# Gated delta rule over two blocks of 128 tokens instead of four chunks of 64, in a streamed-weight decoder layer

## The chip, the cores and the metric

The kernel is one launch on one NeuronCore of a Trainium2 chip. Its engines are TensorE (PE), VectorE (DVE), ScalarE (ACT), GpSimd (POOL) and SyncE (SP), which issues every DMA here. The metric is the device time of that launch in microseconds (us).

## The reference

One decoder layer with batch 1, 256 tokens, width 2048: three residual branches, each fed by a norm that a conditioning vector `c` scales and shifts, and a last norm.

```python
x = x + 0.5 * gt1 * swiglu(ada_in(x, norm_g[0], sh1, sc1), wg[0], wu[0], wd[0])
x = x + gt2 * hybrid_mixer(ada_in(x, norm_g[1], sh2, sc2), w_in, w_out, ...)
x = x + 0.5 * gt3 * swiglu(ada_in(x, norm_g[2], sh3, sc3), wg[1], wu[1], wd[1])
return rmsnorm(x, final_norm)
```

The mixer has 8 heads of softmax attention with a forget gate (FoX) and 8 heads of the gated delta rule, all 128 wide. The delta rule, in chunks of `c` tokens (64 in the reference; the size of the chunk does not change what is computed):

```python
lower = where(strict, (kb @ k.T) * decay, 0)          # per chunk, c x c
t_inv = inverse(eye + lower)
u, w = t_inv @ vb, t_inv @ (kb * exp(g))
a = where(incl, (q @ k.T) * decay, 0)
# over the chunks, in order
v_new = u - w @ state
o = (q * exp(g)) @ state + a @ v_new
state = state * exp(g_last) + (k * exp(g_last - g)).T @ v_new
```

## The kernel before

**The weight stream.** All weights are read once, as 674 blocks of eight 128x128 tiles. For a block, SP issues a DMA of 512 KB (`wraw`), ACT casts it to `whi` (L129), DVE makes the rest `wlo = wraw - whi` (L141), and PE multiplies each tile with the activations in three products, high by high, high by low and low by high (L815 to L817 in the mixer's projections, `pp`; L828 to L830 for those with tokens in the rows, `pv`; L500 to L511 and L591 to L593 in the two feed-forward parts). These products fill PE from end to end. Between weights DVE also computes the conditioning vector's product with its own matrix (`adat`, L267, 142 pieces).

**The mixer's small work.** What the heads need beside the projections is written as Python generators: `gates`, `decays`, `keys`, `solve`, `gdn` (one head of the delta rule), `fox` (one head of attention), `to_out`. `yield 1.4` asks that 1.4 us of stream pass before the generator goes on; each tile of the stream calls `tick(TILE_US)` with 0.35. So between two tiles PE gets a few small fp32 products, called a visit here, with results in one of three PSUM banks (`pss`) and the next visit far enough behind for DVE or ACT to have answered. The Tile framework's scheduler then orders each engine's instructions; `tc.issue_after` pins one behind another.

**One delta head before** (`gdn`, L1047). `solve` inverts the 16x16 diagonal blocks of four heads at once on DVE (L1023, L1024), writes the result to DRAM and reads it back turned (`lt`, L1029; `x<-lt`, L1033, into a part of `x[:, 7]`), and spreads it over masked 64-wide tiles `U0` (L1037). Then `gdn` doubles the inverse twice, 16 to 32 to 64: `pu` (or `put`) holds `U` transposed and `L @ U`; ACT and DVE copy the one half each into `Tm` (L1072, L1073), DVE masks the other into `Z` (L1078), and `pn = Tm.T @ Z` (L1101, L1121) is added to `U`. With the 64-blocks known, `puw` (L1129, L1130) gives `u` and `w`, and a chain goes over four chunks: `po<-st,wq` (L1149), `vz` on DVE (L1150), `po<-vz,At` (L1152), `pst` (L1155), the new state `st` on DVE (L1160). `orw` (L1164, L1165) collects the output.

**Rows of decays.** `fetch_rows` (L941, `x<-rowd`) spreads four heads' rows of cumulated decay over all partitions, into `x[:, 0:4]` or `x[:, 4:8]`, which are free inside the mixer; `decays` makes the masked `Ln` of them (L950, L953). In attention `plog` (L1203) holds logits, DVE takes their maximum `fmx` (L1208, L1210), ACT the exponents (L1212), PE turns the result (`ppt`, L1217) and multiplies it with `v` (`pfo`, L1223 to L1225); its output goes out through `pft` (L1239).

**Norms and end.** `norm_sums` sums squares over partitions on PE (`nsum`, L337) and makes the reciprocal root (L343 to L348); `rb`/`nrow` (L356, L357) spread it, `ht` (L384) and `hs` (L395) give the modulated activations, column by column through `h_upto`. `W.held` is a list of instructions behind which the coming `wlo` are pinned, one each. At the end `final` transposes x back (`pout`, L1350), scales it with the last norm (L1355, L1356) and stores it in four DMAs (L1357).

Of the kernel before, what the change touches and what calls it, by code (L numbers as in the profile page):

```python
# [8 lines left out]
F32 = mybir.dt.float32  # L9
# [20 lines left out]
EPS = 1e-6  # L30
WB = 8
# [125 lines left out]
def layer_kernel(ctx: ExitStack, tc: tile.TileContext, xrow, c, adaw, cols, cst, w, out, order, dbg=None):  # L157
# [77 lines left out]
    ident = L("ident")  # L235

# [92 lines left out]
    def norm_sums(between=lambda _: None, end=lambda _: None):  # L329
# [14 lines left out]
        V.tensor_scalar(hv, ps[:, 0:4:2], -0.5 / D, -0.5 * EPS, ALU.mult, ALU.add)  # L344
# [182 lines left out]
    def residual(ps, j, m_gt, half, one=False):  # L527
# [6 lines left out]
        i = V.scalar_tensor_tensor(x[:, j], ps[:, :T], g, x[:, j], ALU.mult, ALU.add)  # L534
# [112 lines left out]
    def ffn(which, m_gt, early=None):  # L647
        fs = list(range(NF))
        with tc.tile_pool(name=f"hid{which}", bufs=PARTS[which][1] + HIDX) as hp, \
                tc.tile_pool(name=f"more{which}", bufs=1) as more:  # L650
            W.more = more if MORE else None
            for half in range(2):
# [7 lines left out]
                def after(j):  # L660
                    residual(pds.pop(j), j, m_gt, True, half == 1 and j == KD - 1)
# [46 lines left out]
    def features(i):  # L708
# [4 lines left out]
        def moved():  # L713
            return A.copy(x[:, 2 * i : 2 * i + 2], px.rearrange("p (a t) -> p a t", a=2)).ins
# [24 lines left out]
    with tc.issue_after(hold):  # L739
        hold = A.activation(fy, fv, AF.Sqrt, bias=L("eps"), scale=1.0 / D).ins  # L740
    V.tensor_scalar(fh, fv, -0.5 / D, -0.5 * EPS, ALU.mult, ALU.add)
# [33 lines left out]
    def mixer():  # L775
# [67 lines left out]
        U0 = gp.tile([P, NH, 2, 64], F32, name="U0")  # L843

        def gates(ps):
# [42 lines left out]
            for t in range(2):  # L888
                sl = slice(t * P, (t + 1) * P)
                PE.matmul(pr[:NH, T + t * P : T + (t + 1) * P], y[:, t, gdn_], C("tri64"), start=True, stop=True)  # L890
# [3 lines left out]
            for t in range(2):  # L894
                PE.matmul(pcs[:, t, 1], C("tri64"), y[:, t, gdn_], start=True, stop=True)
                PE.matmul(pcs[:, t, 2], C("tru64"), y[:, t, gdn_], start=True, stop=True)
# [8 lines left out]
            V.tensor_tensor(nbeg, colS[:, :, 4], colS[:, :, 2], ALU.mult)  # L905
            V.tensor_scalar(nbt, colS[:, :, 4], -1.0, None, ALU.mult)
            V.tensor_scalar(ng, colS[:, :, 1], -1.0, None, ALU.mult)
# [12 lines left out]
        bh = lambda c_, n: c_.unsqueeze(1).to_broadcast([n, 2, 64])  # L920

        def decay(h):
# [8 lines left out]
            A.activation(gb, gb, AF.Exp)  # L931
            return dd, gb
# [41 lines left out]
        def keys(h):  # L974
# [14 lines left out]
            A.copy(kT[:, 1], pk[:, :T])  # L989
# [7 lines left out]
        def solve(half):  # L997
# [33 lines left out]
            U = x[:, 7, :P].rearrange("p (n i) -> p n i", n=n)  # L1031
            with tc.issue_after(W.last):
                nc.sync.dma_start(U, lt[ht].rearrange("n b (q i) -> (b q) n i", q=16))  # L1033
            yield 5.0
            for q in range(2):
                with tc.issue_after(W.split):
                    V.tensor_tensor(  # L1037
                        U0[:, hs4].rearrange("p h t (b i) -> p (h t) b i", b=4)[:, 4 * q : 4 * q + 4],
                        U[:, 4 * q : 4 * q + 4].unsqueeze(2).to_broadcast([P, 4, 4, 16]),
                        C("blk").unsqueeze(1).unsqueeze(3).to_broadcast([P, 4, 4, 16]), ALU.mult)  # L1040
# [6 lines left out]
        def gdn(h):  # L1047

            kT, q_ = kk.pop(h).bitcast(F32), qv.pop(h).bitcast(F32)
            dec, egb = ups.pop(h)  # L1050
            L_, U = Ln[:, h], U0[:, h]
            yield 5.0 if h < NH - 2 else 3.0

            pv = pss("pvq")
            pg = pss("pkq")
            pu = pss("pu0")
            for t in range(2):
                sl = slice(t * P, (t + 1) * P)
                PE.transpose(pu[:64, sl], U[:, t], ident)
            for t in range(2):  # L1060
                PE.matmul(pu[:, T + t * 64 : T + (t + 1) * 64], L_[:, t], U[:, t], start=True, stop=True)
            for t in range(2):
                sl = slice(t * P, (t + 1) * P)
                PE.transpose(pv[:, sl], q_[:, 1, sl], ident)
                PE.transpose(pv[:, T + t * P : T + (t + 1) * P], q_[:, 0, sl], ident)
            for t in range(2):
                sl = slice(t * P, (t + 1) * P)
                PE.matmul(pg[:, sl], kT[:, 0, sl], q_[:, 0, sl], start=True, stop=True)

            def factor(i, p_):  # L1070
                v_ = p_[:64, :T].rearrange("p (t i) -> p t i", t=2)
                A.copy(Tms[i][:64, :, :64], v_[:, :, :64])  # L1072
                V.tensor_copy(Tms[i][64:, :, 64:], v_[:, :, 64:])  # L1073
                return Tms[i]

            def masked(l, p_):
                Z = m1p.tile([P, 2, 64], F32, name="Z")
                V.tensor_tensor(Z, p_[:, T : T + P].rearrange("p (t i) -> p t i", t=2), bh(C("zm", 64 * l, 64), P), ALU.mult)  # L1078
                return Z

            Tm = factor(0, pu)
            Z = masked(0, pu)

            ssq = tiny.tile([P, 2], F32, name="ssq")
            kbd = m1p.tile([P, 2, 2, P], F32, name="kbd")
            kb, kd = kbd[:, 0], kbd[:, 1]
            vb = m1p.tile([P, 2, P], F32, name="vb")
            At = m1p.tile([P, 2, P], F32, name="At")
            V.tensor_tensor(At, pg[:, :T].rearrange("p (t i) -> p t i", t=2), dec, ALU.mult)
            for t in range(2):  # L1090
                sl = slice(t * P, (t + 1) * P)
# [3 lines left out]
                A.activation(kb[:, t], kT[:, 1, sl], AF.Copy, scale=rb2[:, t, h : h + 1])  # L1095
                A.activation(kd[:, t], kT[:, 1, sl], AF.Copy, scale=colS[:, t, 3, h : h + 1])
            V.tensor_scalar(ssq, ssq, EPS, EPS * HD, ALU.add, ALU.mult)
            yield 1.6
            pn = pss("pn")
            for t in range(2):  # L1100
                PE.matmul(pn[:, t * 64 : (t + 1) * 64], Tm[:, t], Z[:, t], start=True, stop=True)  # L1101
            U2 = m2p.tile([P, 2, 64], F32, name="U")
            V.tensor_tensor(U2, pn[:, :P].rearrange("p (t i) -> p t i", t=2), U, ALU.add)
            U = U2

            wq = m1p.tile([P, 2, 4, 64], F32, name="wq")
            V.tensor_tensor(wq[:, :, 0:4:3, :], q_[:, 0].rearrange("p (t c i) -> p t c i", t=2, c=2),
                            egb.rearrange("p (t c i) -> p t c i", t=2, c=2), ALU.mult)
            yield 1.4
            pu = pss("put")  # L1110
            for t in range(2):
                sl = slice(t * P, (t + 1) * P)
                PE.transpose(pu[:64, sl], U[:, t], ident)
            for t in range(2):
# [376 lines left out]
```

## Time and profile before

| what | value |
|---|---|
| median of three runs | 1937.86 us (1935.78 to 1939.85) |
| profiled execution, its own time | 1940.82 us |
| its span | 1939.0 us |
| granted TensorE clock over the span | 0.996 |
| bytes moved by DMA | 519.58 MB, mean 268 GB/s |
| mixer | about 749 to 1160 us of the span |

The span goes from the first to the last instruction of the profiled execution; the time also holds what lies around it. Busy times of PE are those of pipelined products, whose durations overlap: what a product costs is seen from the distance of two starts. The idle time of an engine is put down to the instruction that released it last. Rows of a timeline give start, duration, engine, line, operation, `output<-inputs`, shape and count, and in brackets the idle time before with its releaser.

### The profile page before, as it was taken

What the parts mean: (1) busy time and instruction counts of PE and PEld (TensorE: products, weight loads), DVE (VectorE), ACT (ScalarE), POOL (GpSimd) and SP (SyncE); (2) the same over time, 40 slices, a digit from 0 to 9 for tenths busy, and PEclk for the clock granted to TensorE, in tenths of its full rate; (3) what the DMA queues carried; (4) which work ended last, traced back from release to release, by engine and by line L of the source; (5) the groups of instructions that cost most, each with busy time, mean ns of one, the idle gap of its engine ahead of it and who ended that gap; (6) DMA issues with size and microseconds to landing.
All of it is one profiled execution on the core that took longest, in us unless ns stands there. A gap on an engine that the chain in (4) does not pass through costs nothing.

```text
span 1939.0 us, 33791 instructions
## 1 busy us (share of the span) xinstructions
PE 1904.8 (98%) x13134; PEld 1776.8 (92%) x13134; DVE 1557.1 (80%) x2412; ACT 1038.4 (54%) x1645; POOL 55.8 (3%) x55
## 2 busy tenths in 40 slices
PE   9999999999999999999999999999999999999998
PEld 7999999988999989989989999999999999999997
DVE  6999978989999998879988888877777656565654
ACT  7434555433445446857656766665554345555553
POOL 0000000000000020000000002000000000000011
PEclk9999999999999999999999999999999999999999
DMA  9988967999999986685667556677777766666663
GB/s 366 351 341 329 331 233 246 397 377 377 367 355 354 359 322 220 208 320 211 235 245 271 201 174 237 213 263 265 268 266 254 238 199 204 197 205 198 205 199 117
DMA packets 129426, 519.58 MB, mean 268 GB/s; under 512 B 18153, under 2 KB 21481, under 8 KB 111089
## 3 DMA queue, kind: packets, MB, share of 16 engines
q1 hardware_dynamic: 129266, 517.42, 74.1%
q8 instruction: 103, 1.69, 0.3%
q14 instruction: 57, 0.47, 0.1%
HBM read 512.89 MB, written 4.47 MB: 267 GB/s over the span
## 4 chain that ended last, share of the span: by engine, by line
PE 77%; DVE 12%; ACT 4%; issue 3%; DMA 2%; SPq 0%; DVEq 0%; POOL 0%; ACTq 0%; POOLq 0%
PE pd L504 13%; PE pg L500 10%; PE pu L500 10%; PE pd L505 7%; PE pu L501 5%; PE pg L501 5%; DVE wlo L141 5%; PE pgu L593 4%; PE pgu L592 4%; PE pgu L591 4%; DVE adat L267 3%; PE po L504 3%; DMA wraw<-in_w_dram 2%; PE pp L815 2%; PE pp L816 2%
## 5 line engine op out<-in xcount | busy, mean ns | idle before, releaser
L141 DVE TENSOR_TENSOR wlo<-wraw,whi 128x1024 fp32r<-128x1024 f32 x674 | 820.0, 1223 | 263.0 <-ACT whi L129 261.7
L129 ACT CAST whi<-wraw 128x1024 fp32r<-128x1024 f32 x674 | 698.3, 1045 | 525.3 <-PE pd L504 141.6
L504 PE MATMUL pd<-hid,whi 128*128 128x512 f32 x1370 | 449.5, 382 | 0.0
L505 PE MATMUL pd<-hid,wlo 128*128 128x256 f32 x1370 | 374.3, 273 | 4.1 <-DVE wlo L141 4.1
L267 DVE CUSTOM_DVE_ANT_0 adat<-adat,cs,colt 128x2048 f32<-128x2048 f32 x142 | 335.4, 2362 | 5.1 <-DMA adat<-in_ada_dram 5.1
L500 PE MATMUL pg<-hs,whi 128*128 128x512 f32 x912 | 302.3, 382 | 0.5 <-DVE shc L451 0.5
L500 PE MATMUL pu<-hs,whi 128*128 128x512 f32 x912 | 302.2, 382 | 0.0
L504 PEld LDWEIGHTS pd<-hid,whi 128*128 128x128 f32 x1370 | 258.8, 189 | 35.7
L505 PEld LDWEIGHTS pd<-hid,wlo 128*128 128x128 f32 x1370 | 262.9, 192 | 7.5 <-DVE wlo L141 7.3
L501 PE MATMUL pu<-hs,wlo 128*128 128x256 f32 x912 | 249.3, 273 | 0.1
L501 PE MATMUL pg<-hs,wlo 128*128 128x256 f32 x912 | 249.2, 273 | 0.0
L593 PE MATMUL pgu<-hs,wlo 128*128 128x256 f32 x896 | 240.3, 278 | 7.0 <-DVE wlo L141 6.6
L591 PE MATMUL pgu<-hs,whi 128*128 128x256 f32 x896 | 244.9, 276 | 0.7 <-ACT whi L129 0.6
L592 PE MATMUL pgu<-hs,whi 128*128 128x256 f32 x896 | 244.3, 276 | 0.0
L500 PEld LDWEIGHTS pg<-hs,whi 128*128 128x128 f32 x912 | 172.4, 189 | 24.7 <-ACT shc L450 0.7
L500 PEld LDWEIGHTS pu<-hs,whi 128*128 128x128 f32 x912 | 172.4, 189 | 23.6
L815 PE MATMUL pp<-hs,whi 128*128 128x256 f32 x656 | 189.5, 290 | 0.6 <-ACT hs L391 0.6
L816 PE MATMUL pp<-hs,whi 128*128 128x256 f32 x656 | 182.0, 278 | 0.0
L817 PE MATMUL pp<-hs,wlo 128*128 128x256 f32 x656 | 181.5, 277 | 0.0
L593 PEld LDWEIGHTS pgu<-hs,wlo 128*128 128x128 f32 x896 | 168.5, 193 | 10.0 <-DVE wlo L141 9.8
L501 PEld LDWEIGHTS pu<-hs,wlo 128*128 128x128 f32 x912 | 175.0, 192 | 1.7 <-DVE wlo L141 1.5
L501 PEld LDWEIGHTS pg<-hs,wlo 128*128 128x128 f32 x912 | 175.1, 192 | 0.8
(341 smaller groups left out, 2639.4 us busy)
## 6 DMA issues: line engine op xcount, KB each, us to landing
wraw<-in_w_dram SPq DMA_DIRECT2D x674, 512.0 KB, 4.5
adat<-in_ada_dram SPq DMA_DIRECT2D x142, 1024.0 KB, 7.8
xr<-in_xr_dram SPq DMA_DIRECT2D x4, 512.0 KB, 5.5
adaf<-in_ada_dram SPq DMA_DIRECT2D x4, 512.0 KB, 8.9
xd<-x SPq DMA_DIRECT2D x4, 512.0 KB, 7.6
rw<-rowd SPq DMA_DIRECT2D x16, 128.0 KB, 7.6
x<-xd SPq DMA_DIRECT2D x4, 512.0 KB, 5.8
out_dram<-o SPq DMA_DIRECT2D x4, 512.0 KB, 3.8
```

The source lines that it names most:

```text
L129: self.cast = self.nc.scalar.copy(self.h, r).ins
L141: lo_ = nc.vector.tensor_tensor(self.l, r, self.h.bitcast(F32), ALU.subtract)
L267: V.tensor_tensor_reduce(t, t, cs, 1.0, L("adab", q, 1), ALU.mult, ALU.add, mod[:, q : q + 1])
L500: PE.matmul(ps, wt[0], both, start=(k == 0), stop=False)
L501: PE.matmul(ps[:, T:], wt[1], part(k, HI), start=False, stop=(k == KD - 1))
L504: PE.matmul(ps, wt[0], act.rearrange("p q (a b) -> p q b a", a=2), start=first, stop=False)
L505: PE.matmul(ps[:, :T], wt[1], woven(act[:, 0]), start=False, stop=last)
L591: PE.matmul(o, wh, part(k, HI), start=first and s == 0, stop=False, skip_group_check=skip)
L592: PE.matmul(o, wh, part(k, LO), start=False, stop=False, skip_group_check=skip)
L593: PE.matmul(o, wl, part(k, HI), start=False, stop=last, skip_group_check=skip)
L815: PE.matmul(pp[i][:, :T], wh, hh, start=(k == 0), stop=False)
L816: PE.matmul(pp[i][:, :T], wh, hl, start=False, stop=False)
```

## The change

The delta rule goes over two blocks of 128 tokens. The inverse is doubled three times (16, 32, 64, 128), each time with transposes and products of full 128 width, and each `Tm` is one copy on ACT and each `Z` one mask on DVE. The products `puw` fall away: the chain is `v0 = U0.T @ vb`, the state `S = k.T @ v0`, `r = vb - beta * exp(g) * (k @ S)` on DVE, `v1 = U1.T @ r`, with the outputs collected in one bank `po`. `U16` is a tile of its own for the small inverses, and each head spreads its part (`U<-U16`) when it begins.

Beside it: `x` is kept doubled (`XS = 2`), so the half of the feed-forward gates needs no instruction `gh`, and constants of the norms and the gain of the mixer's output change in step; the `wlo` that stood ahead of a norm's first modulated column may be pinned behind it; the end computes two instead of four turns ahead of the last `nsum`, and the output is stored as four contiguous parts.

```diff
@@ h_upto
-            hq["one"](hq["next"] - 1)
+            last = hq["one"](hq["next"] - 1)
+            if hq["next"] == 1 and W.held:
+                W.held[-1] = last.ins
@@ residual
-        if half:
-            gh = tiny.tile([P, 1], F32, name="gh")
-            V.tensor_scalar(gh, g, 0.5, None, ALU.mult)
-            g = gh
@@ first columns of x
-            return A.copy(x[:, 2 * i : 2 * i + 2], px.rearrange("p (a t) -> p a t", a=2)).ins
+            return A.activation(x[:, 2 * i : 2 * i + 2], px.rearrange("p (a t) -> p a t", a=2), AF.Copy, scale=XS).ins
@@ keys
-            A.copy(kT[:, 1], pk[:, :T])
+            A.activation(kT[:, 1, :P], pk[:, :P], AF.Copy, scale=colS[:, 0, 3, h : h + 1])
@@ solve
-            U = x[:, 7, :P].rearrange("p (n i) -> p n i", n=n)
             with tc.issue_after(W.last):
-                nc.sync.dma_start(U, lt[ht].rearrange("n b (q i) -> (b q) n i", q=16))
+                nc.sync.dma_start(U16[:, ht], lt[ht].rearrange("n b (q i) -> (b q) n i", q=16))
             yield 5.0
-            for q in range(2):
-                with tc.issue_after(W.split):
-                    V.tensor_tensor(U0[...], U[...], C("blk")..., ALU.mult)
...
@@ gdn
+            def turned(U):
+                pu = pss("pu")
+                for t, sl in enumerate(halves_):
+                    PE.transpose(pu[:, sl], U[:, t], ident)
+                for t in range(2):
+                    PE.matmul(pu[:, T + t * P : T + (t + 1) * P], L_[:, t], U[:, t], start=True, stop=True)
+                return pu
+            def masked(l, pu):
+                Tm, Z = (m1p.tile([P, 2, P], F32, name=n) for n in ("Tm", "Z"))
+                A.copy(Tm, wide(pu[:, :T]))
+                V.tensor_tensor(Z, wide(pu[:, T:]), bc(C("zm", P * l, P)), ALU.mult)
+                return Tm, Z
+            def doubled(U, Tm, Z):
+                pn = pss("pn")
+                for t, sl in enumerate(halves_):
+                    PE.matmul(pn[:, sl], Tm[:, t], Z[:, t], start=True, stop=True)
+                U2 = m2p.tile([P, 2, P], F32, name="U")
+                V.tensor_tensor(U2, wide(pn[:, :T]), U, ALU.add)
+                return U2
...
+            U = doubled(U, Tm, Z)
+            V.tensor_tensor(qe, q_[:, 0, P:], egb, ALU.mult)
+            for l in range(1, 3):
+                yield 1.6
+                Tm, Z = masked(l, turned(U))
+                yield 1.6
+                U = doubled(U, Tm, Z)
             yield 1.6
+            PE.matmul(pw[:, :P], U[:, 0], vb[:, 0], start=True, stop=True)
+            A.copy(v_, pw[:, :P])
+            yield 1.6
+            PE.matmul(pw[:, :P], kT[:, 1, :P], v_, start=True, stop=True)
+            PE.matmul(po[:, :P], At[:, 0], v_, start=True, stop=True)
+            V.tensor_copy(S, pw[:, :P])
+            yield 1.6
+            PE.matmul(pw[:, :P], kT[:, 0, P:], S, start=True, stop=True)
+            PE.matmul(po[:, P:T], qe, S, start=True, stop=False)
+            V.scalar_tensor_tensor(r_, pw[:, :P], rb2[:, 1, h : h + 1], vb[:, 1], ALU.mult, ALU.add)
+            yield 1.6
+            PE.matmul(pw[:, :P], U[:, 1], r_, start=True, stop=True)
+            A.copy(v_, pw[:, :P])
+            yield 1.6
+            PE.matmul(po[:, P:T], At[:, 1], v_, start=False, stop=True)
@@ final
-            nc.sync.dma_start(out[:, :, g * 512 : (g + 1) * 512], o)
+            nc.sync.dma_start(out[g], o)
-            for i, bank in enumerate((pss, pss, pss, psf)):
+            for i, bank in enumerate((pss, pss)):
...
-        for i, bank in ((4, psb), (5, psb), (6, psb)):
+        for i, bank in ((2, pss), (3, psf), (4, psb), (5, psb), (6, psb)):
```

The order of the instructions moves with it at three places. Each row below gives the line, the operation, `output<-inputs` and shape; line numbers of the changed kernel differ by a few.

On SP, where the first four heads' small inverses come back from DRAM (`lt`) and the second four heads' decay rows (`rowd`) are fetched. Before:

```order
L1033 DMA x<-lt 128x8x16
L126 DMA wraw<-in_w_dram 128x1024
L916 DMA rw<-rowd 128x256
L126 DMA wraw<-in_w_dram 128x1024
L941 DMA x<-rowd 128x4x256
```

The same place now:

```order
L1025 DMA U_8249<-lt 128x8x16
L941 DMA x<-rowd 128x4x256
L127 DMA wraw<-in_w_dram 128x1024
L917 DMA rw<-rowd 128x256
L127 DMA wraw<-in_w_dram 128x1024 x2
```

`x<-rowd` has moved ahead of two blocks of weights, directly behind the read of `lt` (`U_8249` is `U16`).

On DVE at the same place, before:

```order
L1037 TENSOR_TENSOR U_8312<-x,cstt 128x256 x2
L141 TENSOR_TENSOR wlo<-wraw,whi 128x1024
L1208 ISA x,fmx<-plog,fm 128x128
L1208 ISA fmx 128x1
L1208 ISA x,fmx<-plog,fm 128x256
L1208 ISA fmx 128x1
L928 TENSOR_TENSOR dec<-cstt,rw 128x256
L1210 TENSOR_SCALAR fmx<-fmx 128x2
L141 TENSOR_TENSOR wlo<-wraw,whi 128x1024
L950 TENSOR_TENSOR Ln<-cstt,x 128x1024
```

And now:

```order
L1043 TENSOR_TENSOR U<-U_8249,cstt 128x256
L950 TENSOR_TENSOR Ln<-cstt,x 128x1024
L1167 ISA x,fmx<-plog,fm 128x128
L1167 ISA fmx 128x1
L1167 ISA x,fmx<-plog,fm 128x256
L1167 ISA fmx 128x1
L1169 TENSOR_SCALAR fmx<-fmx 128x2
L1189 SCALAR_TENSOR_TENSOR fzz<-fzz 128x2
L142 TENSOR_TENSOR wlo<-wraw,whi 128x1024
```

`Ln`, which reads what `x<-rowd` brings, stands ahead of the attention's maxima instead of behind them, and two `wlo` have moved behind them.

On DVE at the mixer's start, before:

```order
L356 TENSOR_SCALAR rb<-colt,nstd 128x128 x2
L141 TENSOR_TENSOR wlo<-wraw,whi 128x1024
L384 SCALAR_TENSOR_TENSOR ht<-x,g_8235,nrow 128x256 x3
L395 SCALAR_TENSOR_TENSOR hs<-ht,mod,hs 128x256 x3
L384 SCALAR_TENSOR_TENSOR ht<-x,g_8235,nrow 128x256 x4
```

And now:

```order
L359 TENSOR_SCALAR rb<-colt,nstd 128x128 x2
L387 SCALAR_TENSOR_TENSOR ht<-x,g_8172,nrow 128x256 x3
L398 SCALAR_TENSOR_TENSOR hs<-ht,mod,hs 128x256 x3
L387 SCALAR_TENSOR_TENSOR ht<-x,g_8172,nrow 128x256 x4
L398 SCALAR_TENSOR_TENSOR hs<-ht,mod,hs 128x256
```

The `wlo` behind `rb` is gone from there; it now stands eight rows, thirteen instructions, further down. On PE at the very end, the order was two instructions of `nsum`, sixteen transposes `pout`, two of `nsum`, sixteen `pout`; now nine `pout` stand ahead of the last `nsum` and 23 behind it.

More of the change, by code (lines that the diff above doesn't have):

```diff
@@ L30 @@
 EPS = 1e-6
+XS = 2.0
 WB = 8
@@ L660, in after @@
                 def after(j):
-                    residual(pds.pop(j), j, m_gt, True, half == 1 and j == KD - 1)
+                    residual(pds.pop(j), j, m_gt, half == 1 and j == KD - 1)
                     if half == 1:
@@ L842, in mixer @@
         Ln = gp.tile([P, NH, 2, P], F32, name="Ln")
-        U0 = gp.tile([P, NH, 2, 64], F32, name="U0")
+        U16 = gp.tile([P, 2 * NH, 16], F32, name="U16")
         def gates(ps):
@@ L1050, in gdn, with spread @@
             dec, egb = ups.pop(h)
-            L_, U = Ln[:, h], U0[:, h]
-            yield 5.0 if h < NH - 2 else 3.0
+            L_ = Ln[:, h]
+            halves_ = [slice(t * P, (t + 1) * P) for t in range(2)]
+            wide = lambda p_: p_.rearrange("p (t i) -> p t i", t=2)
+            yield 3.0 if h < NH - 2 else 1.5
+            def spread():
+                U = m2p.tile([P, 2, P], F32, name="U")
+                V.tensor_tensor(
+                    U.rearrange("p t (b i) -> p t b i", b=8),
+                    U16[:, 2 * h : 2 * h + 2].unsqueeze(2).to_broadcast([P, 2, 8, 16]),
+                    C("blk").unsqueeze(1).unsqueeze(3).to_broadcast([P, 2, 8, 16]), ALU.mult)
+                return U
@@ L1054, in gdn @@
+            def doubled(U, Tm, Z):
[5 more added lines that the diff above has]
+                return U2
+            U = spread()
+            yield 2.0
             pv = pss("pvq")
             pg = pss("pkq")
[L1056 to L1063, printed above, removed]
+            pu = turned(U)
+            for t, sl in enumerate(halves_):
                 PE.transpose(pv[:, sl], q_[:, 1, sl], ident)
                 PE.transpose(pv[:, T + t * P : T + (t + 1) * P], q_[:, 0, sl], ident)
-            for t in range(2):
-                sl = slice(t * P, (t + 1) * P)
+            for sl in halves_:
@@ L1081, in gdn @@
-            Tm = factor(0, pu)
-            Z = masked(0, pu)
+            Tm, Z = masked(0, pu)
             ssq = tiny.tile([P, 2], F32, name="ssq")
-            kbd = m1p.tile([P, 2, 2, P], F32, name="kbd")
-            kb, kd = kbd[:, 0], kbd[:, 1]
             vb = m1p.tile([P, 2, P], F32, name="vb")
             At = m1p.tile([P, 2, P], F32, name="At")
-            V.tensor_tensor(At, pg[:, :T].rearrange("p (t i) -> p t i", t=2), dec, ALU.mult)
-            for t in range(2):
-                sl = slice(t * P, (t + 1) * P)
+            qe = m1p.tile([P, P], F32, name="qe")
@@ L1092, in gdn @@
+            V.tensor_tensor(At, wide(pg[:, :T]), dec, ALU.mult)
+            for t, sl in enumerate(halves_):
                 j2 = tmp.tile([P, P], BF16, name="j1")
@@ L1100, in gdn @@
[L1100 to L1114, printed above, removed]
-                PE.matmul(pu[:, T + t * 64 : T + (t + 1) * 64], L_[:, t], U[:, t], start=True, stop=True)
-            Tm = factor(1, pu)
-            Z = masked(1, pu)
-            yield 1.4
-            pn = pss("pn")
-            for t in range(2):
-                PE.matmul(pn[:, t * 64 : (t + 1) * 64], Tm[:, t], Z[:, t], start=True, stop=True)
@@ L1427, in pack_cols @@
     put("ones", np.ones((P, P), np.float32))
-    put("eps", np.full((P, 1), EPS, np.float32))
+    put("eps", np.full((P, 1), XS * XS * EPS, np.float32))
     return a
@@ L1489 @@
     o = r.results[0]["out_0_dram"]
-    return np.ascontiguousarray(o.transpose(1, 0, 2).reshape(T, D))[None]
+    return np.ascontiguousarray(o.transpose(2, 1, 0, 3).reshape(T, D))[None]
```

123 lines of the change are left out of this document (33 added, 90 removed).

## The prediction, made before the changed kernel ran

> **What bounds the kernel now.** I read the page's busy shares first, then the chain that ended last, then a table of stretches, then the waits of TensorE (PE) in the stretch that the change rewrites.
>
> ```profile
> PE 1904.8 (98%) x13134; PEld 1776.8 (92%) x13134; DVE 1557.1 (80%) x2412; ACT 1038.4 (54%) x1645; POOL 55.8 (3%) x55
> PE 77%; DVE 12%; ACT 4%; issue 3%; DMA 2%; SPq 0%; DVEq 0%; POOL 0%; ACTq 0%; POOLq 0%
> ```
>
> PE is busy 98% of the span and owns 77% of the chain: a PE instruction removed is time removed, and work on other engines counts only through waits. Next the stretches (us, busy time and instructions of PE, weight load, DVE, ACT and POOL, then granted clock, DMA share, GB/s):
>
> ```profile
> 864.00:868.00 4.00, 0.36 (x2) 0.36 (x3) 4.00 (x9) 3.53 (x7) 0.00 (x0) 0.83 0.85 321
> 868.00:872.00 4.00, 4.00 (x21) 4.00 (x21) 2.71 (x4) 2.92 (x10) 0.43 (x2) 0.50 1.01 417
> 876.00:960.00 84.00, 82.16 (x713) 80.31 (x712) 80.64 (x236) 58.47 (x147) 0.00 (x0) 1.00 0.62 219
> ...
> 1060.00:1160.00 100.00, 96.53 (x807) 93.80 (x806) 85.73 (x237) 70.70 (x163) 0.00 (x0) 1.00 0.53 186
> ```
>
> The mixer runs from 749 to 1160 us. PE has a hole at 864 to 868, after which its clock is 0.50; elsewhere it stays full. DVE has 81 of 84 us taken in the first stretch with delta heads, so a DVE result asked for there comes late. PE's waits in the mixer, with the total, how often and the longest:
>
> ```profile
> PE ppt L1217 <- ACT x L1212: 3.7, 1, 3.7
> PE po L1149 <- DVE st L1160: 1.3, 3, 0.6
> PE pn L1101 <- DVE rsa_o L298: 1.1, 1, 1.1
> PE pn L1101 <- DVE Z L1078: 0.9, 2, 0.7
> PE pn L1121 <- DVE Z L1078: 0.8, 2, 0.5
> PE put L1113 <- DVE U L1103: 0.5, 1, 0.5
> PE pn L1121 <- DVE x L1024: 0.5, 1, 0.5
> ```
>
> Only the first is large. The delta rule's own waits are the other six, 5.1 us over eight heads.
>
> **1. PE work of the delta rule.** Its price is read from starts, not from the durations, which overlap:
>
> ```profile
> 921.75 0.38 PE L1113 MATMUL put<-colt,U 128*64 128x128 f32 x2
> 921.97 0.55 PE L1115 MATMUL put<-U,Ln 128*128 128x64 f32 x4
> 922.33 0.36 PE L815 MATMUL pp<-hs,whi 128*128 128x256 f32 x1
> 922.52 0.28 PE L816 MATMUL pp<-hs,whi 128*128 128x256 f32 x1
> ```
>
> From 921.75 to 922.52 stand seven instructions: 0.77 us, 0.110 each. Transposes, the 64-wide products and the 256-wide one of the stream cost the same, so doubling a product's width costs nothing, and I count instructions. A product here is two of them, a transpose one. Before, a head has 56: `pu` 6, `pvq` 4, `pkq` 4, `pn` 4, `put` 6, `pn` 4, `puw` 8, then 20 in the chain over four chunks. After, 52: three rounds of 6 and `pn` 4 make 30, `pvq` and `pkq` 8, and the chain over two blocks 14. Four fewer, eight heads: 32 x 0.111 = **-3.55 us**, all on the path.
>
> **2. DVE and ACT work of the delta rule.** Rows of the mixer, busy time, mean ns, and the idle before:
>
> ```profile
> L1150 DVE TENSOR_TENSOR vz<-u,po 64x128 f32<-64x128 f32 x24 | 6.8, 285 | 3.5 <-PE po L1149 2.7
> L1089 DVE TENSOR_TENSOR At<-pkq,dec 128x256 f32<-128x256 f32 x8 | 3.3, 418 | 0.1
> L1096 ACT ACTIVATE kbd<-kk,colS 128x128 f32<-128x128 f32 x16 | 6.3, 394 | 0.1
> L1134 ACT COPY u<-puw 128x256 f32<-128x256 f32 x8 | 2.9, 368 | 4.7 <-DVE wq L1133 4.6
> L1132 ACT COPY uz<-puw 64x128 f32<-64x128 f32 x8 | 2.1, 258 | 4.6 <-PE puw L1130 4.6
> ```
>
> I price an op at the row of its size. DVE loses per head eleven ops of at most 128 columns (11 x 0.285), two `st`, two `wq` and half a spread of `U0` (4.5 x 0.418): 5.0 us. It gains the spread of `U`, three `Z` and three `U` of 256 columns and `r` (8 x 0.418), `qe` and `S` (2 x 0.285): 3.9. ACT loses four `kb`/`kd` (0.394), `u` and two `orw` (0.368 each) and three small copies (0.258): 3.5; it gains three `Tm` (0.368) and `v0`, `v1` (0.258): 1.6. Both get lighter, by 1.1 and 1.9 us a head. That is hidden behind PE and pays only in waits.
>
> The waits: a head has three `pn` instead of two, each behind a fresh `Z` and `Tm`. The four `pn` rows are 3.3 us in 16 visits, 0.2 each: eight more visits +1.6. `put` is 0.5 in 8 visits: eight more +0.5. The chain has five dependent steps spaced 1.6 where it had seven spaced 1.2 (units of `tick`, which one tile of the stream advances by 0.35): its 1.3 falls to at most 0.9. Bounds: +1.7 by these rows; -5.1 if lighter engines answered in time everywhere. With DVE still 80% busy I stay near the upper end but not on it: **+0.5 us**.
>
> **3. The hole at 864.** It is one train of waits:
>
> ```profile
> 853.61 0.38 SPq L1033 DMA_DIRECT2D x<-lt  x1
> 861.50 0.76 DVE L1037 TENSOR_TENSOR U<-x,cstt 128x256 f32<-128x256 f32 x2 [3.23 <-DMA x<-lt]
> 862.29 0.38 SPq L941 DMA_DIRECT2D x<-rowd  x1
> 862.83 1.05 ACT L129 CAST whi<-wraw 128x1024 fp32r<-128x1024 f32 x1 [5.44 <-DMA wraw<-in_w_dram]
> 867.11 0.39 ACT L1212 ACTIVATE x<-x,fmx 128x128 f32<-128x128 f32 x1
> 867.64 0.47 PE L1217 MATMUL ppt<-colt,x 128*128 128x128 f32 x1 [3.66 <-ACT x L1212]
> ```
>
> `U` waits for its round trip through DRAM. `x<-rowd` writes over part of the tile that `U` reads, so SP stands before it until 862.29; the weights behind it on SP's queue then reach ACT 5.44 us late; the softmax follows, and PE waits 3.66 us. With the hole and the clock at 0.50 behind it (four us at half speed lose two), the event takes some 6 us. After, `U16` has a tile of its own: `x<-rowd` stands right behind `U16<-lt`, held by nothing of `U`, and weights follow at once, so the 5.44 goes. But `Ln<-cstt,x`, 1.2 us of DVE that waits for `x<-rowd`, now stands ahead of the softmax's maximum, and the fox output `pft` 0.6 of a weight block later, by the order. What is late next is DVE: U at 861.5 (same round trip), Ln to 863, the maxima, ACT's table load and exponents, PE again about 2 us idle at `ppt`, then another 2 at the product behind it (estimates from the rows' durations). Ends: -5 us if PE never idles long enough to lose its clock and DVE's later backlog costs nothing, +3 if the hole comes back elsewhere with a half clock. I take **0**.
>
> The Trainium skill, "TensorE: Matmul & The Clock Gate", Part 1 "The HAM clock gate", says that the array falls to half clock after an idle window of about 3.4 us; the trace agrees (3.66 us idle, then 0.50). By that rule two holes of 2 us would keep the full clock, and the sum would be 2 us lower than the one below.
>
> **4. Norm order at the mixer's start.**
>
> ```profile
> 746.86 0.48 DVE L356 TENSOR_SCALAR rb<-colt,nstd 128x128 f32<-128x128 f32 x2
> 747.26 1.22 DVE L141 TENSOR_TENSOR wlo<-wraw,whi 128x1024 fp32r<-128x1024 f32 x1
> 748.39 1.25 DVE L384 SCALAR_TENSOR_TENSOR ht<-x,g,nrow 128x256 f32<-128x256 f32 x3
> 749.46 0.71 PE L815 MATMUL pp<-hs,whi 128*128 128x256 f32 x4 [0.57 <-ACT hs L391]
> 755.13 1.22 DVE L141 TENSOR_TENSOR wlo<-wraw,whi 128x1024 fp32r<-128x1024 f32 x1
> ```
>
> The `wlo` at 747.26 moves behind thirteen norm ops. `ht` still needs `nrow`, two transposes after `rb`, so it gains some 0.6 of the 1.13 us, and so does the first `pp`. The moved `wlo` then ends near 755.0, and its block is due 16 tiles (16 x 0.335) after 748.9, at 754.3 plus visits: half of the gain may be given back. Between -0.6 and +0.5 I take **-0.4 us**.
>
> **5. The end.**
>
> ```profile
> 1926.62 1.95 PE L1350 MATMUL pout<-colt,x 128*128 128x128 f32 x16
> 1927.03 0.42 ACT L316 ACTIVATE sq<-x 128x256 f32<-128x256 f32 x1 [5.89 <-DVE x L534]
> 1928.40 0.50 PE L337 MATMUL nsum<-colt,sq 128*128 128x2 f32 x4
> DMA packets 1088, 2.10 MB, mean 233 GB/s; under 512 B 64, under 2 KB 64, under 8 KB 1088
> q1 hardware_dynamic: 1088, 2.10, 62.6%
> ```
>
> Sixteen transposes fill 1926.62 to 1928.40, 0.111 each, and `nsum` stands behind them though `sq` ends at 1927.45. With nine ahead it starts at 1927.62: -0.78, of which I book 0.65, since seven transposes come later. The last two rows are of 1930 to 1939: the four stores are 1024 packets of 2 KB, and their engines are busy 62.6% of 9 us, 5.6. The two halves of a partition's 4 KB now lie together in DRAM. The 868 row moved weights, 4 KB a partition, at 417 GB/s; at that rate 2.10 MB take 5.0. Between 0 and -0.6 I take -0.35. Together **-1.0 us** (0 to -1.4).
>
> **6. Doubled x.** `gh` leaves DVE, hidden. ACT's eight first copies become activations with a scale, on the way to the first matmul. The mixer has both forms at one size, on PSUM:
>
> ```profile
> L966 ACT COPY cp<-pp 128x256 f32<-128x256 f32 x15 | 5.4, 359 | 0.0
> L1291 ACT ACTIVATE x<-pp 128x256 f32<-128x256 f32 x14 | 5.3, 377 | 0.1
> ```
>
> Seven copies by 18 ns: **+0.1** (0 to +0.3, were it to grow with the width). The wider constants load and the five memsets gone from POOL lie beside other work: 0.
>
> **The sum.** -3.55 + 0.5 + 0 - 0.4 - 1.0 + 0.1 = -4.35. The profiled execution took 1940.82 (span 1939.0) and would take 1936.5; the three runs shown had a median of 1937.86, so the forecast is **1933.5**. What a measurement here can tell from no change is about 0.2%, 3.9 us: faster means below 1934.0.
>
> **Rivals.**
> A. The event shrinks: its holes stay short, the clock stays 1.00, DVE catches up. For: SP no longer stops. Against: DVE, with 81 of the next 84 us taken, has no room to catch up. It gives -4.35 - 3.5, about 1930. Chance 0.25.
> B. All three rounds of `Z` and `Tm` wait: the 24 `pn` at 0.3 instead of 0.2 is +2.4, and the event costs 1 more: 1937. For: DVE 81 of 84. Against: lighter DVE. Chance 0.25.
> C. Slower: `Ln` ahead of the maxima makes the fox head wait for `x<-rowd`. The round trip before it took from 853.61 to 861.50; should `x<-rowd`, a transfer of four rows to all partitions behind it, land after 868, then the maxima come at 869.2, `ppt` at 870.9. The hole is 3.2 us longer, a second stretch at half clock loses 2 more, and DVE's queue, 3.2 late when the first delta head starts, makes that head's `pn` wait by as much: +8.4, so 1942. Against: nothing in front of it on its queue. It decides from a landing at 868 on. Chance 0.12.
> D. The four instructions a head leave PE, but the weights' casts pace the mixer, so only the end moves: 1936.9. Against: PE is 96.5 to 98% full at a DMA share of 0.53 to 0.62. Chance 0.05.
>
> **How the numbers follow.** The forecast has 0.33. Its own range, 1931.5 to 1935.5 by the bounds of steps 2 and 4, puts 0.20 of it below 1934.0 and 0.13 above; A adds 0.25 and the better edge of B 0.05: faster 0.50. Same: 0.13 + 0.20 of B + D 0.05 = 0.38. Slower: C, 0.12. The range runs from A with its lower bound (a further -3) to the upper part of B: 1927 to 1940, which leaves C out and less than 0.1 of the rest.
>
> **What would show it.** PE has 32 instructions fewer in gdn; starts on `pn` of 128 columns stay 0.11 apart (if they took 0.22, step 1 loses all). The waits `pn` from `Z` total 5 to 7 us. At 860 to 885 ACT's 5.44 is gone and PE's holes are 2 us; the clock row tells A from C. `nsum` starts 0.7 us nearer to the last `pd`. A mixer not shorter by 2 us or more makes the prediction wrong.

## The result, and the profile after

The changed kernel took 1926.97 us (median of 6 runs, 1925.01 to 1928.63), the kernel before 1937.59 beside it: a ratio of 0.9945, 95% interval 0.9935 to 0.9955. That is 10.6 us less where 4.35 were forecast, and below the range of 1927 to 1940 by a hair. The profiled execution took 1927.21, its span 1925.4. The page's busy shares and chain now:

```profile
PE 1895.6 (98%) x13102; PEld 1770.6 (92%) x13102; DVE 1540.0 (80%) x2305; ACT 1023.1 (53%) x1603; POOL 54.1 (3%) x50
PE 80%; DVE 11%; ACT 3%; issue 3%; DMA 2%; SPq 0%; DVEq 0%; ACTq 0%
```

The bound is the same; the chain has lost DVE and ACT. PE's waits in the mixer, total, times, longest:

```profile
PE pfo L1182 <- ACT x L1178: 1.6, 1, 1.6
PE ppt L1176 <- ACT x L1171: 1.3, 3, 1.0
PE pft L1198 <- DVE on L1194: 1.2, 2, 0.7
PE pp L818 <- DVE wlo L142: 1.2, 1, 1.2
PE pkq L1080 <- DVE Z L1060: 1.0, 2, 0.7
PE pkq L1080 <- DVE orw L1132: 0.7, 1, 0.7
PE pu L1052 <- DVE U L1068: 0.7, 1, 0.7
PE pn L1066 <- DVE Z L1060: 0.4, 2, 0.2
PE pw L1114 <- DVE S L1111: 0.2, 1, 0.2
```

In place of the wait of 3.7 at `ppt` stand two, 1.0 at `ppt` and 1.6 at `pfo` (0.4 before), and the delta rule's own rows (`pkq`, `pu`, `pn`, `pw`) are 3.0 instead of 5.1. The wait of `pp` for `wlo` is new.

**Where the time went.** All traces record the same 12,342 products of the weight stream, so the n-th of one is the n-th of another, and the time between the same two can be compared. One stretch, from product 6150 to 7600, is seven of the eight delta heads. (The first head begins at product 6006 and is nearly done at 6150.) Its first and last product, before and then after (start, duration):

```profile
909.67 0.36 PE L815 MATMUL pp<-hs,whi 128*128 128x256 f32 x1
1166.04 0.38 PE L504 MATMUL po<-oh,whi 128*128 128x512 f32 x1
```

```profile
904.25 0.28 PE L816 MATMUL pp<-hs,whi 128*128 128x256 f32 x1
1153.98 0.27 PE L510 MATMUL po<-oh,wlo 128*128 128x256 f32 x1
```

256.37 us have become 249.73. In the table, "again" is a second profile of the kernel before, "alone" the two halves of the change run apart, all in us, from differences of such starts:

| stretch (products) | before | again | beside alone | delta alone | after |
|---|---|---|---|---|---|
| start to the first product | 20.96 | 18.82 | 19.07 | 19.02 | 18.98 |
| first feed-forward part, down (2000-5100) | 480.26 | 480.30 | 479.23 | 480.30 | 479.23 |
| mixer's start (5100-5300) | 28.41 | 28.42 | 29.32 | 28.42 | 29.42 |
| keys and values (5300-5880) | 91.88 | 91.88 | 91.88 | 91.40 | 91.41 |
| the hole and the first head (5880-6150) | 49.73 | 47.03 | 51.01 | 45.23 | 46.77 |
| seven heads (6150-7600) | 256.37 | 256.01 | 255.88 | 250.10 | 249.73 |
| output and second feed-forward (7600-12341) | 760.10 | 760.10 | 760.10 | 759.99 | 759.99 |
| last product to the end | 12.90 | 12.90 | 11.38 | 12.94 | 11.38 |

Products 0 to 2000, which the table leaves out, took 238.44 us in both kernels. Most rows repeat to 0.1 us between kernels that have the same instructions there, the seven heads to 0.5, and are the change's or not, at a look. Three do not repeat: the start, which varies by more than 2 us in both kernels; the mixer's start, 28.6 to 29.8 us in the eleven traces that have its new order; and the hole. Over the six traces of before-like kernels taken in all, the hole's row averages 48.8 us (47.0 to 51.0), and 46.5 over the thirteen of after-like ones (45.0 to 50.6). The sum of steps: -6.3 seven heads (against "again"), -0.5 keys, -2.3 hole, -1.5 end, -1.1 first feed-forward part, +1.0 mixer's start: -10.7, against 10.6 between the medians.

### The profile page after: what moved, and what is told of

The parts are those of the page before. It is cut to its first block, busy times and chain, and to the rows that moved or that the text cites. A ratio compares the mean times of both kernels' runs of the same rounds, so it can differ in the third digit from the quotient of the medians.

```text
span 1925.4 us, 33564 instructions
## 1 busy us (share of the span) xinstructions
PE 1895.6 (98%) x13102; PEld 1770.6 (92%) x13102; DVE 1540.0 (80%) x2305; ACT 1023.1 (53%) x1603; POOL 54.1 (3%) x50
## 4 chain that ended last, share of the span: by engine, by line
PE 80%; DVE 11%; ACT 3%; issue 3%; DMA 2%; SPq 0%; DVEq 0%; ACTq 0%
PE pd L509 13%; PE pg L505 10%; PE pu L505 10%; PE pd L510 7%; PE pu L506 5%; PE pg L506 5%; PE pgu L594 4%; DVE wlo L142 4%; PE pgu L592 4%; PE pgu L593 4%; DVE adat L270 3%; PE po L509 3%; PE pp L817 2%; PE pp L816 2%; PE pp L818 2%
```

## Experiments

**Which part of the change.** `c0_again` is the kernel before; `b2_beside_alone` and `d1_delta_alone` are the hunks of the diff for x, norm order and end, and those for the delta rule, applied alone.

> The kernel before, unchanged, profiled a second time, to see which differences between the two traces are not the change's. Theory 1 (the change saved time in the mixer and at the end only): the first matmul of the stream again starts anywhere between 18.9 and 21 us, by how much of the start runs at half clock, and the hole at PE's ppt near 864 us is there again with 3 to 4 us idle and a clock of 0.50 behind it. Rival (the start is 2 us shorter because of the doubled x or the new constants): the first matmul starts at 20.9 us again, and the before kernel never shows 19.

> Only the delta rule's part of the change (two blocks, the own tile U16, the constants), with the end, the norm order and x as before. Theory 1: 3.55 us of PE instructions, about 5 us of waits inside the delta heads and about 3 us at the hole near 864: 10 to 11.5 us below the kernel before. Rival (the prediction's sizes were right and the rest comes from the edits beside it): 3 us below.

> Only the edits beside the delta rule: end, norm order, doubled x. Theory 1: the end gives 1.4 us and the norm order takes 0.9 back, so 0 to 1 us below the kernel before. Rival: these edits carry most of the gain, 5 us or more below.

The kernel before starts its stream at 18.82 us in its second profile, so those 2 us are not the change's. The delta part alone: 1927.54 us, ratio 0.9953 (0.9941 to 0.9966), 9.1 us. The rest alone: 1935.50, ratio 0.9990 (0.9981 to 0.9999), 1.9 us. They add up to the whole.

**The hole.** `e4_own_tile` gives the kernel before only the tile of its own:

```diff
+        U16 = gp.tile([P, 2 * NH, 16], F32, name="U16")
-            U = x[:, 7, :P].rearrange("p (n i) -> p n i", n=n)
+            U = U16[:, ht]
```

> The kernel before with one edit: the small inverses are read back into a tile of their own (U16) instead of a part of x, so that x<-rowd has nothing to wait for; the four chunks of 64 stay. By the order, x<-rowd moves directly behind that read and Ln ahead of the attention's maxima, as in the changed kernel. Theory 1: PE's hole at ppt goes from 3.7 us to about 1.5, the clock stays 1.00, 2.5 to 4 us below the kernel before. Rival (the hole only shrinks because the delta rule's other instructions moved): no change, the hole stays above 3 us.

1935.80 us, ratio 0.9991 (0.9982 to 1.0000): 1.7 us, and no more than the interval allows to call faster. The rows say why so little. First the kernel before, profiled again; then the edits beside alone; then the own tile; then the change. The first three show the spread of `U` on DVE and PE's `ppt`; the last has SP's `x<-rowd`, DVE's `Ln` and PE's second hole beside them:

```profile
857.12 0.76 DVE L1037 TENSOR_TENSOR U<-x,cstt 128x256 f32<-128x256 f32 x2 [0.71 <-DMA x<-lt]
863.63 0.33 PE L1217 MATMUL ppt<-colt,x 128*128 128x128 f32 x1 [1.71 <-ACT x L1212]
```

```profile
860.48 0.76 DVE L1038 TENSOR_TENSOR U<-x,cstt 128x256 f32<-128x256 f32 x2 [3.99 <-DMA x<-lt]
866.62 0.47 PE L1218 MATMUL ppt<-colt,x 128*128 128x128 f32 x1 [4.76 <-ACT x L1213]
```

```profile
860.41 0.76 DVE L1038 TENSOR_TENSOR U<-U,cstt 128x256 f32<-128x256 f32 x2 [3.06 <-DMA U<-lt]
864.51 0.33 PE L1218 MATMUL ppt<-colt,x 128*128 128x128 f32 x1 [1.99 <-ACT x L1213]
```

```profile
851.21 1.12 SPq L941 DMA_DIRECT2D x<-rowd  x1
858.51 0.42 DVE L1043 TENSOR_TENSOR U<-U,cstt 128x256 f32<-128x256 f32 x1 [2.29 <-DMA U<-lt]
859.93 1.23 DVE L950 TENSOR_TENSOR Ln<-cstt,x 128x1024 f32<-128x1024 f32 x1 [0.99 <-DMA x<-rowd]
862.49 0.33 PE L1176 MATMUL ppt<-colt,x 128*128 128x128 f32 x1 [0.98 <-ACT x L1171]
866.34 0.49 PE L1182 MATMUL pfo<-x 128*128 128x128 f32 x2 [1.58 <-ACT x L1178]
```

When the small inverses come back from DRAM is a draw: DVE waits for them 0.7 to 4.0 us here, and the hole is 1.7 to 4.8 us in one and the same order of instructions. What the own tile changes is the way from `U` to `ppt`: 6.51 and 6.14 us without it, 4.10 and 3.98 with it (6.1 to 6.9 in the six traces without it, 4.0 to 5.1 in the fourteen with it). The second hole at `pfo` takes part of that back.

Most of what the hole's row gained is clock. In all six traces without the own tile the granted clock fell to a half at the hole, for 3.41 or 6.83 us, even where DVE had waited only 0.5 us for the data (y5 below). Of the fourteen with it, it fell in three, those where DVE waited 3.1 us or more (`e4_own_tile`, and n10 and p9 below); in the eleven with waits up to 2.3 us it stayed full. So the profile of `e4_own_tile` is of a late draw (us, busy time and instructions of PE, weight load, DVE, ACT and POOL, then granted clock, DMA share, GB/s):

```profile
862.84:866.25 3.41, 1.58 (x12) 1.39 (x13) 1.21 (x7) 2.69 (x10) 0.42 (x2) 1.00 1.03 423
866.25:869.67 3.42, 2.21 (x12) 1.91 (x10) 1.69 (x3) 3.26 (x7) 0.00 (x0) 0.50 0.42 174
```

Half of 3.41 or 6.83 us is 1.7 or 3.4 us lost at most; that makes 2.6 us on average in the six before-like traces and 0.4 in the thirteen after-like ones. The difference of 2.2 us, an estimate, is close to the 2.3 of the row.

**Price of the PE instructions.** `p9_four_back` writes the two products `pkq` twice per head.

> The changed kernel with each head's two products q by k made twice, which puts back four PE instructions per head, 32 in all, and nothing else. Both theories: 32 x 0.111 = 3.55 us slower than the changed kernel (about 1930.5). Rival (the visits have slack that swallows them): 1 us or less.

Ratio 0.9954 (0.9941 to 0.9968), 1929.92 us, beside 0.9945 for the change: too close for timing. In the seven heads it is 252.34 against 249.73: 2.6 us for 28 instructions, 0.093 each where 0.111 was forecast. The price holds to a sixth.

**Why the heads wait less: gaps or load.** `y5_before_wide` sets `yield 1.4` and `yield 1.2` in the kernel before's `gdn` to 1.6; `y6_after_tight` sets 1.6 to 1.3 in the changed one; `l7_loads` adds, after the doublings of each head,

```diff
+            V.tensor_tensor(dv, dec, dec, ALU.add)   # three per head
+            A.copy(da, dec)                          # five per head
```

> The kernel before, with the five gaps of 1.4 and 1.2 inside a delta head asked at 1.6, as the changed kernel has them; instructions and their number unchanged. Theory S (the delta heads wait less because every dependent visit stands 1.6 behind the last instead of 1.2 to 1.4): the waits at pn, at po after st and at po after vz fall from some 10 us to 5 in the mixer, and the time by 3 to 5 us. Theory L (they wait less because DVE and ACT have 1.1 and 1.9 us less to do per head): the waits stay, the time is that of the kernel before within 1 us, or longer where heads run late.

> The changed kernel with the eight gaps of 1.6 inside a delta head cut to 1.3. Theory S: the waits of the delta heads come back, 3 to 5 us slower than the changed kernel (1930 to 1932). Theory L: within 1 us of the changed kernel (1926 to 1928).

> The changed kernel with work added per delta head that nothing waits for: three DVE additions of 128x256 (about 0.3 to 0.4 us each) and five ACT copies of 128x256 (about 0.4 each), close to the 1.1 and 1.9 us that the change took from these engines. Theory L: the waits come back, 3 to 5 us slower than the changed kernel (1930 to 1932). Theory S: at most 1.5 us slower.

| kernel | time, us | ratio to before (95%) | seven heads, us | products 6150 to 7700, us |
|---|---|---|---|---|
| before, again | | | 256.0 | 272.4 |
| y5, before with 1.6 | 1938.51 | 1.0000 (0.9992 to 1.0009) | 255.5 | 273.7 |
| the change | 1926.97 | 0.9945 (0.9935 to 0.9955) | 249.7 | 266.0 |
| y6, the change with 1.3 | 1934.11 | 0.9980 (0.9971 to 0.9989) | 257.1 | 273.5 |
| l7, the change with loads | 1929.20 | 0.9950 (0.9937 to 0.9962) | 251.5 | 267.7 |

The last column goes 100 products further, because the last head of some versions is late: in y5 its `pot` stands behind product 7600 and waits 0.73 us there, and in the other traces of this table nothing of it does. The first profile of the kernel before has 272.7 us there.

In `l7` the added rows show that they ran:

```profile
L1103 DVE TENSOR_TENSOR dv<-dec 128x256 f32<-128x256 f32 x16 | 6.7, 419 | 0.2
L1104 ACT COPY da<-dec 128x256 f32<-128x256 f32 x15 | 6.2, 410 | 0.2
```

1.26 us of DVE and 2.0 of ACT per head bring back 1.7 us, and that is one wait:

```profile
912.88 0.49 PE L1080 MATMUL pkq<-qv,kk 128*128 128x128 f32 x2 [1.66 <-DVE Z L1060]
```

Tight gaps bring back 7.4, more than the change gave there. Up to 1.7 of these (half of 3.41, an estimate) is a stretch of half clock from 912.87 to 916.29, behind a wait of 1.25 at `pft`; no other trace has one in these heads. But wide gaps do not give anything to the kernel before: to product 7700, y5 takes 1.0 to 1.3 us more. Neither theory stands alone.

**Which gaps.** `y12_chain_tight` sets only the changed chain's four gaps to 1.2, `y13_inverse_tight` only the inverse's six to 1.3; `y14_before_inverse_wide` and `y16_before_chain_wide` set the kernel before's three gaps of 1.4, and its chain's of 1.2, to 1.6.

> The changed kernel with only the four gaps between the chain's visits (v0, S, r, v1) at 1.2 instead of 1.6. Theory S (spacing decides, and most of it in the chain, where four and more dependent answers of DVE and ACT follow each other): the waits of pw and po rise by 3 us or more in the mixer. Rival (the inverse decides): under 1 us more.

> The changed kernel with only the six gaps of the inverse's doublings at 1.3 instead of 1.6. Theory S with most of it in the inverse (every pu waits for DVE's U, every pn for DVE's Z and ACT's Tm, behind weights of 1.2 us each): the waits of pu and pn rise by 4 us or more. Rival (the chain decides): under 1.5 us more.

> The kernel before with only the three gaps of 1.4 in the inverse's part of a delta head at 1.6; the chain keeps its 1.2. Theory S1 (the changed kernel's doublings wait less because their gaps are wider): the waits at pn and put fall from 6 us to 4 or less and the stretch of seven heads gets 1.5 to 2.5 us shorter. Theory S2 (they wait less because each step is two answers, Tm on ACT and Z on DVE, instead of three with a copy on DVE behind one on ACT): these waits stay above 5 us.

> The kernel before with only the chain's seven gaps of 1.2 at 1.6. Theory S1: the waits at po and pst fall from 4.4 us to 2 or less. Theory S3 (seven answers in a row cost what they cost, and only fewer of them help): they stay at 4 us or grow, since a longer head runs into the next.

Seven heads: y12 250.2, y13 251.9, y14 255.6, y16 255.6; to product 7700: 266.4, 268.3, 271.9, 273.5. Ratios 0.9960, 0.9962, 0.9999, 0.9995. In the changed kernel the inverse's gaps matter (2.2 us) and the chain's hardly (0.4), but both at once cost 7.4, or some 5.7 without the half clock, so they do not add; no run shows why.

Gaps come out in whole tiles of 0.35: 1.2 and 1.3 are always four, 1.6 is always five, and 1.4 is four or five as the rounding falls. In y14 every visit of the first five delta heads stands between the same two products as in the kernel before, so there its 1.4 had been five tiles already, and the edit moved visits in the last three heads alone. S1 is thus hardly tested for the inverse. For the chain it fell: y16 did widen it, and `po` waited 2.3 us for `st` where it had waited 1.3.

**Steps of the chain.** `x17_two_more_steps` is y12 with v0 and S sent through PE once more:

```diff
+            PE.matmul(pw[:, :P], ident, v_, start=True, stop=True)
+            V.tensor_copy(va, pw[:, :P])
+            yield 1.2
```

`x18_steps_and_loads` adds the loads of `l7` to it (one DVE addition, five ACT copies).

> The changed kernel with the chain's gaps at 1.2 and two dependent visits more per head: v0 and S are each sent once through PE (a product with the identity) and copied out by DVE before the chain goes on. That makes seven answers in the chain, as the kernel before had, and four PE instructions more per head. Against the changed kernel with the same gaps (y12): the 32 instructions cost 3.3 us by themselves (in p9 they cost 2.6 in the stretch of seven heads). Theory S3 (each dependent answer costs a wait of its own, 0.2 us on average, whatever the gap): 16 visits more add 2 to 4 us beyond that, the time is 1932 to 1935. Rival (only the PE instructions count, the waits come from elsewhere): 1930.5 to 1932.

> The version with two dependent steps more (seven answers in the chain at 1.2, and as many PE instructions per head as the kernel before) with work added that nothing waits for: per head one DVE addition and five ACT copies of 128x256, so that with the two copies already added DVE and ACT have some 1.0 and 2.0 us more per head, as in the kernel before. What the change removes besides its own form is thus put back. In the stretch of seven heads the steps made 253.4 us and the loads alone 251.5, against 249.7 in the changed kernel and 256.0 before. Theory (the PE instructions, the chain's answers and the load on DVE and ACT together are the gain of the delta rule, and the waits add up): 255 to 256.5 us in that stretch. Rival (they do not add up, or something else in the chunked form waits): 254 us or less.

x17: 1931.42 us, ratio 0.9973 (0.9964 to 0.9983), seven heads 253.4; x18: 1931.39, 0.9964 (0.9951 to 0.9976), 253.4 again. But in both, as in y5 and y16, the last head ends late, behind product 7600. In x17:

```profile
1157.01 0.33 PE L1153 MATMUL pot<-colt,orw 128*128 128x128 f32 x1 [0.45 <-DVE orw L1144]
```

From there to product 12341 they take 761.7 and 761.6 us, y12 760.0. So they are compared up to product 7700: 271.3 us both, where y12 has 266.4 and the kernel before 272.4 and 272.7. Of x17's 4.9 us over y12, 3.0 to 3.6 are its 32 instructions at 0.093 to 0.111; its sixteen answers are left with 1.3 to 1.9. On top of them the loads cost nothing. With the kernel before's number of PE instructions, its chain of seven answers and its load, the two-block form is only 1.1 to 1.4 us faster than the chunked one: of the 6.4 to 6.7 us that the change gave up to product 7700, these three put back 5.3. With the 1.7 us behind product 7600 counted in, x18 reaches the 255 us of its theory, though the load has no part in it.

**The smaller edits.** `g11_gh_back` puts `gh` back (a product with 1.0) ahead of the feed-forward residuals; `n10_no_norm` takes out the three lines of `h_upto`; `t12_rows_apart` stores the output as before.

> The changed kernel with one instruction of DVE put back ahead of each column of the feed-forward parts' residual (gh, a product with 1.0 of one number per partition, 0.149 us). In the traces the first feed-forward part's down projection is 1.07 us shorter without it. Theory (gh stood in front of a wlo for which PE waits): that stretch is 1.07 us longer again, the rest unchanged. The prediction's view (hidden): no difference.

> The changed kernel with the wlo at the mixer's start left where the kernel before had it, ahead of the first ht. From the two traces the moved wlo costs PE a wait of 1.2 us at 757 us and gives 0.6 at the first pp. Theory: 0.9 us faster than the changed kernel (about 1926.0), and the wait pp from wlo is gone. The prediction's view: 0.4 us slower than the changed kernel.

> The changed kernel with the output stored as before, 2 KB apart, and the new order of nsum kept. In the traces the part behind the last product of the stream fell from 12.90 to 11.38 us. If the order gives 0.8 and the stores 0.7, it is 12.1 here; if the stores give nothing, 11.4.

`gh` was not hidden: products 2000 to 5100 take 480.31 us with it and 479.23 without. The page's row of the down products, before, after and g11, has PE's wait for `wlo` at its end:

```profile
L505 PE MATMUL pd<-hid,wlo 128*128 128x256 f32 x1370 | 374.3, 273 | 4.1 <-DVE wlo L141 4.1
```

```profile
L510 PE MATMUL pd<-hid,wlo 128*128 128x256 f32 x1370 | 374.3, 273 | 3.0 <-DVE wlo L142 2.9
```

```profile
L510 PE MATMUL pd<-hid,wlo 128*128 128x256 f32 x1370 | 374.3, 273 | 4.1 <-DVE wlo L142 4.1
```

The norm order costs. After the change, DVE's rows and PE's:

```profile
744.75 1.26 DVE L387 SCALAR_TENSOR_TENSOR ht<-x,g,nrow 128x256 f32<-128x256 f32 x3 [0.42 <-PE nrow L360]
750.72 1.22 DVE L142 TENSOR_TENSOR wlo<-wraw,whi 128x1024 fp32r<-128x1024 f32 x1
745.83 0.71 PE L816 MATMUL pp<-hs,whi 128*128 128x256 f32 x4
763.96 0.38 PE L818 MATMUL pp<-hs,wlo 128*128 128x256 f32 x1 [1.21 <-DVE wlo L142]
```

`ht` starts 0.9 us after `rb` instead of 1.53 (748.39 after 746.86), so the first `pp` comes 0.6 earlier. But DVE now idles 0.42 for `nrow` where it made a `wlo`, runs behind PE, and at 763.96 PE waits 1.21. n10 has 28.41 us in this stretch, as before, and lost its 1.0; the keys and values of its trace were 1.2 longer with a wait at `pkk`, which z15 below, with the same start, does not repeat (0.3). Its time is 1926.22, ratio 0.9945 (0.9932 to 0.9959): 1 us cannot be told from none there.

At the end t12 needs 12.17 us: of 1.52, 0.73 is the order and 0.79 the stores, now half as many packets. The rows of 9 us around the stores, t12 and then the change:

```profile
q1 hardware_dynamic: 1088, 2.10, 62.5%
```

```profile
q1 hardware_dynamic: 576, 2.10, 58.4%
```

**A version meant to beat both.** `z15_best` is n10 with the inverse's gaps at 1.75 and the chain's at 1.4.

> A version meant to beat both: the changed kernel without the moved wlo at the mixer's start, with the inverse's six gaps at 1.75 and the chain's four at 1.4 (the chain lost only 0.4 us at 1.2, the inverse 2.2 at 1.3). Theory S: 1 us from the start and 0.5 to 1.5 us from the inverse's waits, 1924.5 to 1926 where the changed kernel has 1927. Rival (at 1.6 the answers already come in time and a wait is where a visit meets a long DVE instruction): within 1 us of the changed kernel.

1928.36 us, ratio 0.9948 (0.9935 to 0.9960), seven heads 251.1: not better than the change. (1.75 is five or six tiles, 1.4 four or five.) Of 1.3, 1.6 and these, 1.6 is the best spacing tried.

## Why the prediction was right or wrong

Step 1 held: 32 instructions at 0.093 to 0.111, 3.0 to 3.55 us, and 128 columns cost what 64 did.

Step 2 failed, and it is the largest miss. It took the waits of the delta heads as +0.5 by counting visits at the mean wait of the present rows; they are about -3 (6.3 us in seven heads less some 2.6 to 3.1 of instructions). PE's idle time, summed from product 6150 to 7700, fell from 6.5 us (both traces of the kernel before) to 4.0. Two of its terms were wrong. Eight more visits each at `pn` and at `pu` were to cost 2.1, and the waits of `pn` for `Z` to total 5 to 7: they total 0.4, with 1.0 at `pkq` behind `Z` and 0.7 at `pu`: 2.1 together, where `pn` and `put` had 3.8 before. And two answers fewer in the chain were to save 0.4: x17 prices them at 1.3 to 1.9. The lower bound of -5.1 was right to be there, and the choice near the upper end wrong: a wait does not belong to a kind of visit. Load on DVE and ACT is not what carries it: it cost nothing in x18 and one wait in l7. Nor do wider gaps in the old chain help. That the old form takes 1.1 to 1.4 us more at equal numbers is measured; which of its instructions does it (half-width copies split over ACT and DVE, or the order in which its answers meet long `wlo` and `adat`) was not tried apart and stays open.

Step 3 was too timid: 0 was taken, -2.3 was measured, on the way of rival A: the clock mostly stays full. The order was read rightly, `Ln` and the second hole included; what was missed is that the way from `U` to `ppt` shortens by 2 us whenever the data arrives. The event was also larger than booked: four us at half clock were counted, and in that trace it lasted 6.83 (866.62 to 873.44). That the time came out near A's lower bound of 1927 is partly luck: A had its gain at the hole alone, and most of it came from the heads. Rival C's price never fell due: DVE waited only 0.99 for `x<-rowd`. The changed kernel's profile shows no half clock there:

```profile
861.00:865.00 4.00, 2.62 (x20) 2.04 (x18) 1.03 (x7) 3.46 (x13) 0.43 (x2) 1.00 1.01 420
865.00:869.00 4.00, 2.67 (x23) 2.67 (x24) 3.03 (x5) 4.00 (x12) 0.00 (x0) 1.00 0.50 171
```

Step 4 had the wrong sign: -0.4 forecast, +1.0 measured (0.2 to 1.4 over the eleven traces with the new order). The gain of 0.6 at the first `pp` was exact; the giving back was looked for at the moved block alone, and came ten microseconds later, from all of DVE's queue. Step 5 was -1.0 against -1.5: the stores gave 0.79, above its bound of 0.6. Step 6 booked `gh` as hidden, and it was worth 1.1: the waits of `pd` for `wlo`, 4.1 us, were on the page, and it stood in front of some of them. The scaled copies at the start could not be seen under its spread of more than 2 us. B and D fell: the waits did not grow, and the instructions' time left the mixer.

## What to carry to other kernels

Where an in-order engine is 80% busy and another waits for it now and then, price an edit by what stands in front of each awaited instruction, not by the mean of a group: 0.15 us ahead of a `wlo` was worth 1.1 in all, and a `wlo` moved back by thirteen small ones cost 0.2 to 1.4. Profile the old kernel twice before explaining a difference: here two places of 2 and 4 us were a draw. Compare stretches between the same two products of the stream; most repeat to 0.1 us where whole runs spread over 5. But let such a stretch end only where no version has work left over: ended at product 7600, four versions here looked 1.5 to 1.8 us better than they were. And look up in the order what a requested gap came out as, before an experiment is built on it.

## What the runs showed of the hardware

The clock does not need an idle stretch as long as 3.66 us to fall. In the second profile of the kernel before, the hole at `ppt` was 1.71 us, and the clock of the next stretch was 0.58 all the same:

```profile
860.00:864.00 4.00, 2.29 (x21) 2.09 (x19) 3.07 (x9) 3.54 (x7) 0.00 (x0) 1.00 0.86 290
864.00:868.00 4.00, 4.00 (x22) 3.88 (x21) 3.32 (x4) 3.06 (x11) 0.42 (x2) 0.58 1.01 414
```

In the changed kernel two holes of 0.98 and 1.58 us cost no clock. The clock's changes in a trace lie 3.41 us or a multiple of it apart. The window of that length ahead of the fall in this second profile, and the least busy one at the changed kernel's holes, which cost nothing:

```profile
861.22:864.63 3.41, 1.70 (x15) 1.38 (x14) 2.48 (x6) 2.82 (x7) 0.00 (x0) 1.00 0.94 353
864.68:868.10 3.42, 1.84 (x16) 1.77 (x16) 2.13 (x3) 3.42 (x11) 0.00 (x0) 1.00 0.44 178
```

PE was busy half of the time in the one and 0.54 in the other. With all twenty traces divided into such windows (start and end left out), each of the 21 windows with PE busy 0.40 or less was followed by half clock and none with 0.51 or more; of seven between 0.44 and 0.50, three were. Half clock ended after a window in which PE was busy 0.85 or more, and went on after the five with 0.35 to 0.73, which is why it lasted 3.41 us in some traces and 6.83 in others. The ends of products are modelled, so these shares are rough. So the rule as the prediction took it from the Trainium skill ("TensorE: Matmul & The Clock Gate", Part 1 "The HAM clock gate") is too kind here: a window in which PE was idle for half of the time was enough.
